# Two LayerNorms of a decoder layer: added products while the statistics run, the order of the first feature pairs, and the last norm as a rounded five-row product

## Chip, cores, metric

One NeuronCore of a Trainium2 chip runs the whole layer in one launch. The metric is the device time of one execution in microseconds (us), as the median of several runs. The engines are TensorE (PE; its weight loads are listed as PEld), VectorE (DVE), ScalarE (ACT), GpSimd (POOL) and SyncE (SP, here a DMA queue only).

## What is computed

A decoder layer on 256 tokens of width 2048 in float32: a token mixer with two branches, then a SwiGLU. Each half ends in a LayerNorm over the 2048 features of a token, and the input of the second half is scaled and shifted feature by feature:

```python
def layer_norm(x, gain, bias):
    mu = xf.mean(-1, keepdims=True)
    var = jnp.square(xf - mu).mean(-1, keepdims=True)
    return ((xf - mu) * lax.rsqrt(var + LN_EPS) * gain + bias).astype(x.dtype)
...
        x = layer_norm(DEEPNORM_ALPHA * x + g1 * y, ln1_g[l], ln1_b[l])
        h = x * (1.0 + sc2) + sh2
        y = swiglu(h, w_ffn_in[l], w_ffn_out[l])
        x = layer_norm(DEEPNORM_ALPHA * x + g2 * y, ln2_g[l], ln2_b[l])
```

## The kernel before

Every float32 product is made of three rounded ones. A weight tile of 128x1024 numbers comes by DMA (`load_w`, line 201), ACT rounds it to `hi` (line 211) and DVE makes `lo = raw - hi` (line 212). PE multiplies hi by the high and the low part of the other operand and lo by its high part (`ws_mm`, lines 289 to 291, weight stationary, 24 products a tile; `xs_unit`, lines 337 to 339, activations stationary). Raw tiles, hi and lo have four buffers each: the conversion of a fifth tile waits until PE is done with the first.

The work is a list of steps. `step` adds one with a weight tile, `do` one without, and `run(3)` goes through the list and issues load and conversion of up to three further tiles ahead of the step that uses them. Behind it a scheduler sets the order of each engine's instructions; `tc.high_priority` lets a piece go ahead of others, and `tc.keep_in_program_order` pins an instruction. At run time every engine takes its own instructions strictly in the order that this gives.

The change touches two places.

The first norm lies between the output projection (`out_unit`, last product of the token mixer) and the first stage of the SwiGLU. `resid` (line 1007) takes a finished block of columns out of PSUM for both halves of the tokens: times the gate (1011), plus alpha times the residual (1012), block statistics (1013). `stats` (1015) joins the blocks' statistics (1020) and takes a reciprocal root with one Newton step (`rsqrt`, lines 347 to 353, of which 348 on ACT). `norm2(g)` (1079) normalizes four features of 128 columns, in pairs: subtract and scale (1084, DVE), four transposes on PE (1090) into one PSUM tile for the pair, then for each feature the scaled and shifted high part (1093, ACT) and the same unrounded (1095, DVE), and one subtraction that gives the low part of the pair (1097). The following stage goes through 4 groups of four features and, in each, through four weight tiles (gate and up, two column blocks each); `norm2(g + 1)` is issued with the first tile of group g.

The end: the last matrix stage ends with `resid` on five blocks of columns (three of 512, two of 256) of the second half's output. After it come `stats` and, for four blocks of 512 columns and both halves of the tokens, a scaling and shift on ACT (1205), times gain (1207) and plus bias (1208) on DVE, of which the last one of each on POOL, and one DMA for each block (1209). Gain and bias of this norm are loaded by SP spread over all 128 partitions, 1 MB each, when the last stage begins (`fo_begin`, lines 1183 and 1184). There also the gate is spread: a transpose (990), a copy (992), and two DMAs on POOL's queue, the write of `rd` (994) and its spread read (995).

Of the kernel before, what the change touches and what calls it, by code (L numbers as in the profile page):

```python
# [10 lines left out]
F32 = mybir.dt.float32  # L11
# [81 lines left out]
def layer(ctx, tc, a, out):  # L93
# [113 lines left out]
    def split_w(raw, kn, cn):  # L207
# [4 lines left out]
        v_.tensor_tensor(lo, raw, hi.bitcast(F32), op=OP.subtract)  # L212
# [50 lines left out]
    def step(w, k0, kn, c0, cn, post):  # L263
        prog.append((lambda: split_w(load_w(w, k0, kn, c0, cn), kn, cn), post))

    def do(fn):
        prog.append((None, fn))

    def run(ahead):
        n = out = 0  # L270
        ready = {}
        for i, (pre, post) in enumerate(prog):
# [734 lines left out]
    def resid(ps, c0, cn, gb, base, dst, st, n):  # L1007
        cc = slice(c0, c0 + cn)
        for h in range(2):
            t = wp.tile([P, 512], F32, tag="acc", name="rt", bufs=2)[:, :cn]  # L1010
            v_.tensor_tensor(t, ps[h], gb[:, cc], op=OP.mult)
            v_.scalar_tensor_tensor(dst[:, h, cc], base[:, h, :], ALPHA, t, op0=OP.mult, op1=OP.add)
            v_.bn_stats(st[:, h, n, :], dst[:, h, cc])

    def stats(st):
        mv = perm.tile([P, 2, 2], F32, tag="mv", name="mv", bufs=2)
        rs = perm.tile([P, 2, 1], F32, tag="lrs", name="lrs", bufs=2)
        with tc.high_priority(offset=400):
            for h in range(2):
                v_.bn_aggr(mv[:, h, :], st[:, h])  # L1020
            rsqrt(rs, *[perm.tile([P, 2, 1], F32, tag="l" + n, name="l" + n) for n in "er"], mv[:, :, 1:2], epsc[:, 1:2])
# [20 lines left out]
    def out_unit(n, c0, cn):  # L1042
# [6 lines left out]
        xs_unit(m_ops, w_o, c0, KT, lambda ps: resid(ps, c0, cn, cur["g1b"], cur["xs"], cur["r"], cur["st"], n), cn)  # L1049
# [10 lines left out]
    def ffn_begin():  # L1060
        halves = [perm.tile([P, 8, 2, S], F32R, tag=tag, name="h2") for tag in ("s0", "s1")]
        cur["h2"] = halves
        for k in range(KT):
            h2.append(halves[k // 8][:, k % 8])
            for x in range(2):
                h2_ops[x].append(h2[k][:, x, :])
        p1.close()
# [7 lines left out]
        cur["mv"], cur["rs"] = stats(cur["st"])  # L1075
# [3 lines left out]
    def norm2(g):  # L1079
        r, mv, rs = cur["r"], cur["mv"], cur["rs"]  # L1080
        for f in range(4 * g, 4 * g + 4, 2):
# [4 lines left out]
            tp = pt.tile([P, 2, S], F32, tag="tp", name="tp")  # L1086
# [4 lines left out]
            t = cur["h2"][f // 8][:, f % 8:f % 8 + 2]  # L1091
# [152 lines left out]
```

## Time and profile before

| | us |
|---|---|
| three runs | 1791.91, 1789.39, 1779.66 |
| their median | 1789.39 |
| the profiled execution | 1785.36 |
| its span, first to last instruction | 1783.6 |
| mean granted clock of TensorE in it | 0.983 of full speed |

The profile is of one execution; its rows give the start from the span's start and the duration in us. Outside the span lie 1.8 us of the profiled execution. A product's duration holds the time in which the next one already runs, so the distance of two starts is what one costs.

### The profile page before, as it was taken

The numbers are of one execution on the slowest core, as the hardware profiler recorded it, in microseconds if no ns is written. First come the engines' busy times: TensorE is split into PE (matmuls) and PEld (weight loads), VectorE is DVE, ScalarE is ACT, GpSimd is POOL, SyncE is SP. The second block draws the span as 40 slices with busy tenths as digits, with TensorE's granted clock in tenths as the row PEclk, the third lists the DMA queues.
The fourth block names the chain that finished last, engine by engine and source line by source line (L and its number), as shares of the span: only waits on it lengthen the run. The fifth ranks groups of instructions, "written<-read, shape, count | busy, mean of one in ns | idle before, by whom it ended". The sixth has DMA issues, their size and how long they took to land.

```text
span 1783.6 us, 28261 instructions
## 1 busy us (share of the span) xinstructions
PE 1686.6 (95%) x11149; PEld 1537.1 (86%) x11149; DVE 1249.9 (70%) x1786; ACT 815.2 (46%) x1118; POOL 49.9 (3%) x68
## 2 busy tenths in 40 slices
PE   3899999999989999899999899999999999999995
PEld 3899999979989788889998899888888888888895
DVE  6899988888856787657875677676666655455454
ACT  3544445667433445336344344544444444433342
POOL 0000000110100001000000000000000000000001
PEclk9999999999999999999999999999999999999998
DMA  9999887666677577876876647777777755765652
GB/s 356 331 339 353 345 310 227 199 196 189 205 238 238 186 237 247 271 239 206 296 265 222 191 129 245 251 252 239 238 246 232 242 193 192 258 197 188 197 185 82
DMA packets 115158, 421.56 MB, mean 236 GB/s; under 512 B 13456, under 2 KB 14384, under 8 KB 109392
## 3 DMA queue, kind: packets, MB, share of 16 engines
q1 hardware_dynamic: 110016, 402.21, 66.7%
q0 software_dynamic: 5008, 17.53, 3.7%
q8 instruction: 88, 1.44, 0.3%
q14 instruction: 46, 0.38, 0.1%
HBM read 412.27 MB, written 7.42 MB: 235 GB/s over the span
## 4 chain that ended last, share of the span: by engine, by line
PE 41%; issue 15%; DMA 8%; DVE 5%; ACT 1%; POOL 0%; POOLq 0%; DVEq 0%; ACTq 0%
PE mm L296 16%; PE mm L300 8%; DMA raw_a<-in_w_ada 4%; DVE lo L212 3%; PE mm L290 3%; PE mm L291 3%; PE mm L289 3%; PE mm L339 2%; PE mm L338 2%; PE mm L337 2%; DMA raw<-in_w_proj_gdn 2%; DMA raw<-in_w_in 1%; ACT hi L211 1%; PE ps L691 1%; DMA rb<-rnd 1%
## 5 line engine op out<-in xcount | busy, mean ns | idle before, releaser
L211 ACT CAST hi<-raw 128x1024 fp32r<-128x1024 f32 (+2 forms) x572 | 582.0, 1020 | 768.7 <-PE mm L339 210.7
L212 DVE TENSOR_TENSOR lo<-raw,hi 128x1024 fp32r<-128x1024 f32 (+2 forms) x572 | 672.8, 1183 | 286.1 <-ACT hi L211 282.1
L289 PE MATMUL mm<-s,hi 128*128 128x256 f32 x1184 | 338.9, 286 | 4.9 <-ACT hi L211 4.7
L291 PE MATMUL mm<-s,lo 128*128 128x256 f32 x1184 | 333.3, 283 | 6.3 <-DVE lo L212 6.2
L290 PE MATMUL mm<-s,hi 128*128 128x256 f32 x1184 | 332.5, 281 | 0.0
L296 PE MATMUL mm<-h,hi 128*128 128x512 f32 x1280 | 319.0, 391 | 0.0
L296 PEld LDWEIGHTS mm<-h,hi 128*128 128x128 f32 x1280 | 228.8, 188 | 39.5
L289 PEld LDWEIGHTS mm<-s,hi 128*128 128x128 f32 x1184 | 225.0, 190 | 10.8 <-ACT hi L211 7.5
L291 PEld LDWEIGHTS mm<-s,lo 128*128 128x128 f32 x1184 | 224.2, 190 | 9.4 <-DVE lo L212 8.5
L290 PEld LDWEIGHTS mm<-s,hi 128*128 128x128 f32 x1184 | 224.8, 190 | 0.4
L300 PEld LDWEIGHTS mm<-h,lo 128*128 128x128 f32 x1280 | 171.1, 188 | 13.2
L300 PE MATMUL mm<-h,lo 128*128 128x256 f32 x1280 | 174.1, 278 | 0.0
L337 PE MATMUL mm<-hi,ach 128*128 128x512 f32 (+1 forms) x440 | 152.6, 347 | 0.0
L338 PE MATMUL mm<-lo,ach 128*128 128x512 f32 (+1 forms) x440 | 152.5, 347 | 0.0
L339 PE MATMUL mm<-hi,acl 128*128 128x512 f32 (+1 forms) x440 | 152.5, 347 | 0.0
L229 DVE CUSTOM_DVE_ANT_0 raw_a<-raw_a,cb,cols 128x1024 f32<-128x1024 f32 x56 | 71.8, 1283 | 77.9 <-DMA raw_a<-in_w_ada 77.9
L229 DVE CUSTOM_DVE_ANT_0 raw_a<-raw_a,cb,ada_half 128x1024 f32<-128x1024 f32 x56 | 71.8, 1283 | 64.8 <-DMA raw_a<-in_w_ada 64.8
L229 DVE CUSTOM_DVE_ANT_0 r<-r,cb,cols 128x2048 f32<-128x2048 f32 x40 | 93.7, 2347 | 14.1 <-DMA r<-in_w_ada 14.1
L337 PEld LDWEIGHTS mm<-hi,ach 128*128 128x128 f32 x440 | 83.3, 189 | 10.4
L339 PEld LDWEIGHTS mm<-hi,acl 128*128 128x128 f32 x440 | 83.3, 189 | 10.4
L338 PEld LDWEIGHTS mm<-lo,ach 128*128 128x128 f32 x440 | 83.3, 189 | 10.1
L338 PE MATMUL mm<-lo,s 128*128 128x512 f32 x192 | 77.0, 401 | 2.2 <-DVE lo L212 2.2
(288 smaller groups left out, 2383.2 us busy)
## 6 DMA issues: line engine op xcount, KB each, us to landing
raw<-in_w_ffn_in SPq DMA_DIRECT2D x176, 512.0 KB, 4.3
raw<-in_w_in SPq DMA_DIRECT2D x168, 512.0 KB, 4.4
raw_a<-in_w_ada SPq DMA_DIRECT2D x112, 512.0 KB, 4.5
raw<-in_w_ffn_out SPq DMA_DIRECT2D x88, 512.0 KB, 4.3
r<-in_w_ada SPq DMA_DIRECT2D x40, 1024.0 KB, 7.6
raw<-in_w_proj_gdn SPq DMA_DIRECT2D x32, 512.0 KB, 4.5
raw<-in_w_out SPq DMA_DIRECT2D x32, 512.0 KB, 4.2
raw<-in_w_in SPq DMA_DIRECT2D x40, 384.0 KB, 5.8
```

Source lines behind the costliest of these rows:

```text
L211: s_.copy(hi, raw)
L212: v_.tensor_tensor(lo, raw, hi.bitcast(F32), op=OP.subtract)
L229: v_.tensor_tensor_reduce(out=raw, in0=raw, in1=cb[:, n * part:n * part + n], scale=1.0, scalar=cols[:, col:col + 1] if first else h, op0= ...
L289: t_.matmul(o, hi[:, i, c], ah, start=(first and i == 0 and t == 0), stop=False)
L290: t_.matmul(o, hi[:, i, c], al, start=False, stop=False)
L291: t_.matmul(o, lo[:, i, c], ah, start=False, stop=(last and i == kn - 1 and t == 1))
L296: t_.matmul(box[t].rearrange("p (u i) -> p u i", u=2), hi[:, i, t * P:(t + 1) * P], both[k0 + i], start=(first and i == 0), stop=False)
L300: t_.matmul(box[t][:, :S], lo[:, i, t * P:(t + 1) * P], both[k0 + i][:, 0, :], start=False, stop=(last and i == kn - 1))
L337: t_.matmul(box[h], xh, hi[:, i, :], start=start, stop=False)
L338: t_.matmul(box[h], xh, lo[:, i, :], start=False, stop=False)
L339: t_.matmul(box[h], xl, hi[:, i, :], start=False, stop=stop)
L691: t_.matmul(ps[:lt.shape[1], n, :], lt, rt, start=True, stop=True)
```

## The change

At the first norm: the last block's `resid` and the statistics behind it are issued as one piece with high priority (`then`). Sixteen products of a finished tile with itself, 512 columns wide, whose result nobody reads, stand on PE behind the last product of the output projection. The two features of a pair get a PSUM tile each, and DVE takes the second feature first. The first two weight tiles are multiplied with the first two features for both tiles (`ws_some`: first everything that needs only high parts, then the rest) before the other two features come in, and `norm2(1)` is issued with the second tile. The fourth tile is loaded and converted no earlier than the first step of the stage (`begun`), with its `lo` pinned (`pin`).

At the second norm: the bias no longer comes spread over the partitions. Gain and bias come once more as rows of 16 x 128, are split into a high and a low part (ACT and DVE), written to DRAM and read back as a tile of five rows: gain high, gain low, bias high, bias low, gain high. Each finished block of columns is multiplied by the gain, once its statistics are taken. At the end the mean times the reciprocal root, negated and split, and ones make a five-row operand for each half of the tokens (two transposes, one copy). One rounded product per half block gives -mean * rs * gain + bias in PSUM, and one DVE step adds r * rs. The last block goes out in two DMAs.

```diff
-    def split_w(raw, kn, cn):
+    def split_w(raw, kn, cn, pin=False):
...
-        v_.tensor_tensor(lo, raw, hi.bitcast(F32), op=OP.subtract)
+        low = v_.tensor_tensor(lo, raw, hi.bitcast(F32), op=OP.subtract)
+        if pin:
+            tc.keep_in_program_order(low)
...
-            while n < len(prog) and (n <= i or out <= ahead):
+            while n < len(prog) and (n <= i or (out <= ahead and prog[n][2] <= i)):
...
-    def resid(ps, c0, cn, gb, base, dst, st, n):
+    def resid(ps, c0, cn, gb, base, dst, st, n, then):
         cc = slice(c0, c0 + cn)
...
+        last = c0 + cn == D
+        with tc.high_priority(offset=400 if last else 0):
+            for h in range(2):
...
+            if last:
+                then(*stats(st))
...
+        keep = pg.tile([P, 512], F32, tag="gd", name="keep")
+        for _ in range(16):
+            t_.matmul(keep, cur["mh"][0][:, 0, :P], cur["mh"][0][:, 0:2, :], start=True, stop=True)
         p1.close()
...
+            t = cur["h2"][f // 8][:, f % 8:f % 8 + 2]
+            tps = []
             for i in range(2):
+                tps.append(pt.tile([P, S], F32, tag="tp", name="tpn"))
                 for h in range(2):
-                    t_.transpose(tp[:, i, h * P:(h + 1) * P], r[:, h, (f + i) * P:(f + i + 1) * P], ident)
+                    t_.transpose(tps[i][:, h * P:(h + 1) * P], r[:, h, (f + i) * P:(f + i + 1) * P], ident)
...
+                j = 1 - i
+                v_.tensor_scalar(hf[:, j, :], tps[j], sa[:, 0, f + j:f + j + 1], sa[:, 1, f + j:f + j + 1],
                                  op0=OP.mult, op1=OP.add)
...
+    def ws_some(ps, hi, lo, some, first, last):
+        for i in some:
+            for t in range(2):
+                o, c = ps[:, t * S:(t + 1) * S], slice(t * P, (t + 1) * P)
+                t_.matmul(o, hi[:, i, c], h2_ops[0][i], start=(first and i == some[0] and t == 0), stop=False)
+                t_.matmul(o, lo[:, i, c], h2_ops[0][i], start=False, stop=False)
+        for i in some:
+            for t in range(2):
+                t_.matmul(ps[:, t * S:(t + 1) * S], hi[:, i, t * P:(t + 1) * P], h2_ops[1][i], start=False, stop=False)
...
-                if n == 0 and g < 3:
-                    norm2(g + 1)
-                ws_mm(pss[n], h2_ops, hi, lo, 4 * g, 4, g == 0, g == 3)
...
+                held.append((hi, lo))
+                ws_some(pss[n], hi, lo, (0, 1), True, False)
+                if n:
+                    norm2(1)
+                    for m in range(2):
+                        ws_some(pss[m], *held[m], (2, 3), False, False)
...
-        dma.dma_start(b1[:, 1, :], a["ln2_b"][0].partition_broadcast(P))
...
+        row = wp.tile([KT, 2, P], F32, tag="acc", name="row", bufs=2)
+        for i, v in enumerate(("ln2_g", "ln2_b")):
+            sdma.dma_start(row[:, i, :], a[v].rearrange("o (k p) -> (o k) p", p=P))
+        hl = wp.tile([KT, 2, 2, P], F32R, tag="acc", name="hl", bufs=2)
+        split(hl[:, 0], hl[:, 1], row)
+        hld = dr.tile([4, D], F32R, name="hld")
+        sdma.dma_start(hld.rearrange("x (k p) -> k x p", p=P), hl.rearrange("k x v p -> k (x v) p"))
+        rows = cur["rows"] = k3.tile([5, D], F32R, name="rows")
+        sdma.dma_start(rows[0:4], hld)
+        sdma.dma_start(rows[4:5], hld[0:1])
...
+            resid(ps, c0, cn, cur["g2b"], r[:, :, cc], r, cur["st"], n, finish)
+            for h in range(2):
+                v_.tensor_tensor(r[:, h, cc], r[:, h, cc], cur["g"][:, cc], op=OP.mult)
...
+    def finish(mv, rs):
...
+        v_.scalar_tensor_tensor(nm, mv[:, :, 0:1], -1.0, rs, op0=OP.mult, op1=OP.mult)
+        v_.tensor_copy(z[:, :, 0:3:2], nm.to_broadcast([P, 2, 2]))
+        v_.tensor_tensor(z[:, :, 4:5], nm, z[:, :, 0:1].bitcast(F32), op=OP.subtract)
+        tp = pt.tile([P, 512], F32, tag="tp", name="tpm")
+        for h in range(2):
+            t_.transpose(tp[0:5, h * P:(h + 1) * P], z[:, h, :].bitcast(F32), ident)
...
+        s_.copy(zt, tp[0:5, :S].rearrange("p (h i) -> p h i", h=2))
...
-            s_.activation(r[:, h, cc], r[:, h, cc], AF.Identity, bias=nm[:, h], scale=rs[:, h])
-            e = g_ if (n == 3 and h == 1) else v_
-            e.tensor_tensor(r[:, h, cc], r[:, h, cc], b1[:, 0, cc], op=OP.mult)
-            e.tensor_tensor(r[:, h, cc], r[:, h, cc], b1[:, 1, cc], op=OP.add)
...
+            t_.matmul(ps, cur["zt"][:, h], cur["rows"][:, cc], start=True, stop=True)
+            v_.scalar_tensor_tensor(r[:, h, cc], r[:, h, cc], rs[:, h], ps, op0=OP.mult, op1=OP.add)
```

Three places show what the scheduler makes of it. In the names, `lo<-raw,hi` is the low part of a weight tile, `rt`, `r`, `st`, `mv` and `lrs` are the steps of a block and of its statistics, and `tp` or `tpn` is a transposed pair or feature. A line number that begins a row is that of its own kernel, those of after being later by what was added above.

DVE at the first norm, before, from the second half of the last block to the third pair:

```order
L1012 SCALAR_TENSOR_TENSOR r<-xs,rt 128x256
L1020 BN_AGGR mv<-st_9708 128x2
L212 TENSOR_TENSOR lo<-raw,hi 128x1024
L1013 BN_STATS st_9708<-r 128x6
L1020 BN_AGGR mv<-st_9708 128x2
...
L1097 TENSOR_TENSOR h_10446<-hf_10474,h_10446 128x2x256
L1084 TENSOR_SCALAR r<-r,mv,lrs 128x256 x2
L1095 TENSOR_SCALAR hf_10487<-tp,sa 128x256 x2
L1097 TENSOR_TENSOR h_10446<-hf_10487,h_10446 128x2x256
L1084 TENSOR_SCALAR r<-r,mv,lrs 128x256 x2
```

And DVE at the same place after:

```order
L1016 SCALAR_TENSOR_TENSOR r<-xs,rt 128x256
L1025 BN_AGGR mv<-st_9708 128x2
L1017 BN_STATS st_9708<-r 128x6
L1025 BN_AGGR mv<-st_9708 128x2
...
L1107 TENSOR_TENSOR h_10453<-hf_10484,h_10453 128x2x256
L1092 TENSOR_SCALAR r<-r,mv,lrs 128x256 x2
L1105 TENSOR_SCALAR hf_10498<-tpn,sa 128x256 x2
L1107 TENSOR_TENSOR h_10453<-hf_10498,h_10453 128x2x256
L212 TENSOR_TENSOR lo<-raw,hi 128x1024 x2
L1092 TENSOR_SCALAR r<-r,mv,lrs 128x256 x2
```

The low part of the fourth tile has moved from within the statistics to behind the second pair, where another one follows it, ahead of the third pair's normalization.

ACT where the last matrix stage begins, before (`ach` is the high part of the last SwiGLU activations):

```order
L1114 COPY up<-mm 128x256 x2
L211 CAST hi<-raw 128x1024
L217 CAST ach<-up 128x512
L211 CAST hi<-raw 128x1024 x65
```

And ACT there after:

```order
L1124 COPY up<-mm 128x256 x2
L211 CAST hi<-raw 128x1024
L219 CAST ach<-up 128x512
L219 CAST hl<-row 16x256
L211 CAST hi<-raw 128x1024 x65
```

The split of the two rows stands ahead of all conversions of the stage but the first of these.

DVE at the last block of the last norm, before:

```order
L1011 TENSOR_TENSOR rt<-mm,b_15073 128x256
L1012 SCALAR_TENSOR_TENSOR r<-r,rt 128x256
L1013 BN_STATS st_15084<-r 128x6
L1020 BN_AGGR mv<-st_15084 128x2
L347 TENSOR_SCALAR le<-mv,epsc 128x2
```

And DVE there after (`b_15099` is the gain):

```order
L1015 TENSOR_TENSOR rt<-mm,b_15098 128x256
L1238 TENSOR_TENSOR r<-r,b_15099 128x256
L1016 SCALAR_TENSOR_TENSOR r<-r,rt 128x256
L1017 BN_STATS st_15121<-r 128x6
L1025 BN_AGGR mv<-st_15121 128x2
L1238 TENSOR_TENSOR r<-r,b_15099 128x256
L349 TENSOR_SCALAR le<-mv,epsc 128x2
```

Both multiplications by the gain of the last block stand within the chain that ends in the reciprocal root.

## Rows read from the trace of the kernel before

**Rows 1.** The page: the span, and from its first section TensorE's busy time in us (share of the span) and number of instructions.

```profile
span 1783.6 us, 28261 instructions
...
PE 1686.6 (95%) x11149; PEld 1537.1 (86%) x11149; DVE 1249.9 (70%) x1786; ACT 815.2 (46%) x1118; POOL 49.9 (3%) x68
```

**Rows 2.** Busy time by window (us from the span's start): length, then PE, PEld, DVE, ACT and POOL busy us (instructions), PE's granted clock, the DMA engines' busy share and GB/s. The first norm in three stretches, the last matrix stage, the end.

```profile
1018.95:1024.30 5.35, 0.17 (x3) 0.01 (x1) 4.84 (x16) 1.25 (x2) 0.00 (x0) 0.81 0.59 194
1024.30:1032.50 8.20, 6.29 (x26) 5.45 (x27) 3.23 (x7) 2.03 (x4) 0.00 (x0) 0.50 0.00 2
1032.50:1079.90 47.40, 46.97 (x393) 46.04 (x392) 35.61 (x54) 24.61 (x32) 0.00 (x0) 1.00 0.53 167
1531.00:1764.00 233.00, 233.00 (x1278) 203.78 (x1276) 113.49 (x109) 86.80 (x83) 0.51 (x1) 1.00 0.57 185
1764.00:1783.60 19.60, 0.18 (x2) 0.00 (x0) 11.65 (x27) 5.96 (x9) 6.03 (x2) 0.56 0.28 107
```

**Rows 3.** PE's timeline around the first norm: start, duration, line, operation, out<-in, shape, count, and in brackets the engine's idle time ahead of it with what ended it. The last row is the first product of the stage that follows.

```profile
1018.83 0.28 PE L339 MATMUL mm<-hi,ml 128*128 128x256 f32 x1
1024.30 1.23 PE L1090 MATMUL tp<-cst,r 128*128 128x128 f32 x4 [5.18 <-DVE r L1084]
1026.17 1.23 PE L289 MATMUL mm<-h,hi 128*128 128x256 f32 x4 [0.66 <-ACT h L1093]
1028.66 0.58 PE L290 MATMUL mm<-h,hi 128*128 128x256 f32 x1 [1.26 <-DVE h L1097]
...
1031.17 0.41 PE L291 MATMUL mm<-h,lo 128*128 128x256 f32 x1
1031.38 0.41 PE L289 MATMUL mm<-h,hi 128*128 128x256 f32 x1
...
1033.09 0.28 PE L290 MATMUL mm<-h,hi 128*128 128x256 f32 x1
1033.21 0.28 PE L291 MATMUL mm<-h,lo 128*128 128x256 f32 x1
...
1079.90 1.32 PE L296 MATMUL mm<-h,hi 128*128 128x512 f32 x5
```

**Rows 4.** DVE's timeline at the same place.

```profile
1020.48 1.16 DVE L212 TENSOR_TENSOR lo<-raw,hi 128x1024 fp32r<-128x1024 f32 x1
1021.56 0.42 DVE L1013 BATCH_NORM_STATS2 st<-r 128x6 f32<-128x256 f32 x1
...
1023.83 0.73 DVE L1084 TENSOR_SCALAR r<-r,mv,lrs 128x256 f32<-128x256 f32 x2
1026.16 0.54 DVE L1095 TENSOR_SCALAR hf<-tp,sa 128x256 f32<-128x256 f32 x1 [1.59 <-ACT h L1093]
1027.33 0.55 DVE L1095 TENSOR_SCALAR hf<-tp,sa 128x256 f32<-128x256 f32 x1 [0.63 <-ACT h L1093]
1027.91 0.69 DVE L1097 TENSOR_TENSOR h<-hf,h 128x512 fp32r<-128x512 f32 x1
```

**Rows 5.** ACT's timeline at the same place.

```profile
1025.56 0.56 ACT L1093 ACTIVATE h<-tp,sa 128x256 fp32r<-128x256 f32 x1 [2.76 <-PE tp L1090]
1026.73 0.56 ACT L1093 ACTIVATE h<-tp,sa 128x256 fp32r<-128x256 f32 x1 [0.61 <-DVE hf L1095]
...
1036.61 1.05 ACT L211 CAST hi<-raw 128x1024 fp32r<-128x1024 f32 x1 [0.19 <-PE mm L290]
```

**Rows 6.** PE's timeline at an earlier gap in dense work, and the window around it with the columns of rows 2.

```profile
134.57 0.39 PE L291 MATMUL mm<-s,lo 128*128 128x256 f32 x1 [1.57 <-DVE lo L212]
...
130.00:137.00 7.00, 5.43 (x46) 5.23 (x45) 6.31 (x8) 2.17 (x3) 0.00 (x0) 1.00 0.86 297
```

**Rows 7.** Where the last matrix stage begins: POOL's timeline (DMA issues), ACT's, PE's (the first product of the stage), and the time from issue to landing of line 994's two DMAs.

```profile
1523.78 0.51 POOL L994 DMA_DIRECT2D rd<-rw  x1 [587.09 <-DVE rw L992]
1530.96 0.55 POOL L995 DMA_DIRECT2D b<-rd  x1 [6.67 <-ACT hi L211]
...
1526.83 1.05 ACT L211 CAST hi<-raw 128x1024 fp32r<-128x1024 f32 x1 [1.19 <-issue]
...
1521.05 0.48 PE L337 MATMUL mm<-hi,ach 128*128 128x512 f32 x1
...
DMA to landing us min/median/max: 3.9/5.3/6.6
```

**Rows 8.** The end: DVE's and POOL's timelines, the four DMAs of the output (line 1209; durations of the issue in ns, first and last start, time from issue to landing), and a window with the columns of rows 2.

```profile
1766.01 0.23 DVE L347 TENSOR_SCALAR le<-mv,epsc 128x2 f32<-128x2 f32 x1
...
1767.50 0.16 DVE L1201 SCALAR_TENSOR_TENSOR nm<-mv,lrs 128x2 f32<-128x2 f32 x1
...
1769.88 1.28 DVE L1207 TENSOR_TENSOR r<-r,b 128x512 f32<-128x512 f32 x2
...
1773.54 4.77 POOL L1207 TENSOR_TENSOR r<-r,b 128x512 f32<-128x512 f32 x1 [242.03 <-ACT r L1205]
1778.38 1.26 POOL L1208 TENSOR_TENSOR r<-r,b 128x512 f32<-128x512 f32 x1
...
L1209 SPq DMA_DIRECT2D out<-r x4: 372/384/398, 1771.8 to 1779.7; - x4
...
DMA to landing us min/median/max: 2.7/2.8/2.8
...
1773.00:1774.00 1.00, 0.00 (x0) 0.00 (x0) 1.00 (x2) 0.45 (x1) 0.46 (x1) 0.50 1.02 387
```

More of the change, by code (lines that the diff above doesn't have):

```diff
@@ L261, in layer, with step @@
     prog = []
-    def step(w, k0, kn, c0, cn, post):
-        prog.append((lambda: split_w(load_w(w, k0, kn, c0, cn), kn, cn), post))
+    def step(w, k0, kn, c0, cn, post, begun=0, pin=False):
+        prog.append((lambda: split_w(load_w(w, k0, kn, c0, cn), kn, cn, pin), post, begun))
     def do(fn):
-        prog.append((None, fn))
+        prog.append((None, fn, 0))
     def run(ahead):
@@ L271, in run @@
         ready = {}
-        for i, (pre, post) in enumerate(prog):
-            while n < len(prog) and (n <= i or out <= ahead):
+        for i, (pre, post, _) in enumerate(prog):
+            while n < len(prog) and (n <= i or (out <= ahead and prog[n][2] <= i)):
                 if prog[n][0]:
@@ L1005, in layer @@
     do(out_begin)
-    def resid(ps, c0, cn, gb, base, dst, st, n):
+    def resid(ps, c0, cn, gb, base, dst, st, n, then):
         cc = slice(c0, c0 + cn)
[L1009 to L1013, printed above, removed]
+        last = c0 + cn == D
+        with tc.high_priority(offset=400 if last else 0):
+            for h in range(2):
+                t = wp.tile([P, 512], F32, tag="acc", name="rt", bufs=2)[:, :cn]
+                v_.tensor_tensor(t, ps[h], gb[:, cc], op=OP.mult)
+                v_.scalar_tensor_tensor(dst[:, h, cc], base[:, h, :], ALPHA, t, op0=OP.mult, op1=OP.add)
+                v_.bn_stats(st[:, h, n, :], dst[:, h, cc])
+            if last:
+                then(*stats(st))
     def stats(st):
@@ L1017, in stats @@
         rs = perm.tile([P, 2, 1], F32, tag="lrs", name="lrs", bufs=2)
[L1018 to L1021, printed above, removed]
+        for h in range(2):
+            v_.bn_aggr(mv[:, h, :], st[:, h])
+        rsqrt(rs, *[perm.tile([P, 2, 1], F32, tag="l" + n, name="l" + n) for n in "er"], mv[:, :, 1:2], epsc[:, 1:2])
         return mv, rs
@@ L1129, in wide_unit @@
             step(w_fi, k, 4, c0, 256, post)
+    def ws_some(ps, hi, lo, some, first, last):
[7 more added lines that the diff above has]
+                t_.matmul(ps[:, t * S:(t + 1) * S], hi[:, i, t * P:(t + 1) * P], h2_ops[1][i], start=False, stop=False)
+    begun, held = len(prog), []
     for g in range(4):
@@ L1133, in post @@
             def post(hi, lo, g=g, n=n):
-                if n == 0 and g < 3:
-                    norm2(g + 1)
-                ws_mm(pss[n], h2_ops, hi, lo, 4 * g, 4, g == 0, g == 3)
-            step(w_fi, 4 * g, 4, o, 256, post)
+                if g or n > 1:
+                    if n == 0 and g < 3:
+                        norm2(g + 1)
+                    ws_mm(pss[n], h2_ops, hi, lo, 4 * g, 4, g == 0, g == 3)
+                    return
+                held.append((hi, lo))
[4 more added lines that the diff above has]
+                        ws_some(pss[m], *held[m], (2, 3), False, False)
+            step(w_fi, 4 * g, 4, o, 256, post, begun if (g, n) >= (0, 3) else 0, (g, n) == (0, 3))
     def ln1_affine():
@@ L1180, in fo_begin @@
         b0 = perm.tile([P, 2, D], F32, tag="s0", name="b0")
[L1181 removed]
+        b1 = perm.tile([P, 1, D], F32, tag="s1", name="b1")
         bcast_row(5, b0[:, 0, :])
         dma.dma_start(b1[:, 0, :], a["ln2_g"][0].partition_broadcast(P))
[L1184 to L1185 removed]
+        cur["g2b"], cur["g"] = b0[:, 0, :], b1[:, 0, :]
+        k3 = cur["k3"]
+        row = wp.tile([KT, 2, P], F32, tag="acc", name="row", bufs=2)
[8 more added lines that the diff above has]
+        sdma.dma_start(rows[4:5], hld[0:1])
+        z = cur["z"] = k3.tile([P, 2, 5], F32R, name="z")
+        v_.memset(z.bitcast(F32), 1.0)
         cur["st"] = perm.tile([P, 2, 5, 6], F32, tag="stt", name="st2", bufs=2)
```

34 lines of the change are left out of this document (18 added, 16 removed).

## The prediction

> **What bounds the kernel now.** I read the page's busy times first, then windows, then the engines' timelines around both norms. TensorE (PE) is busy 1686.6 of 1783.6 us [rows 1], and in the last matrix stage it never stops (233.00 of 233.00 us) while VectorE (DVE) is busy 113.49 [rows 2]: what does not hold PE up there costs nothing. So only the two places where PE does stop can pay.
>
> At the first norm the last product of the output projection starts at 1018.83 and PE sits idle 5.18 us until the row statistics and the first normalization are done [rows 3]. Its granted clock falls in that gap (mean 0.81), is 0.50 from 1024.3 to 1032.5, so the lower level of 1.2 GHz, and 1.00 (2.4 GHz) after [rows 2]. Products start every 0.21 us at the lower clock (1031.17 to 1031.38) and every 0.12 at the higher (1033.09 to 1033.21) [rows 3]. In the slow stretch PE waits twice more: 0.66 us for ScalarE (ACT) and 1.26 us for DVE [rows 3].
>
> At the end PE is out of work at 1764.0 and the span ends at 1783.6: 19.6 us of DVE, ACT, POOL and one transfer [rows 2, 8].
>
> **The first norm, step by step.** From 1032.5 to 1079.9 PE is held up hardly at all: 47.40 us with 393 instructions [rows 2], 0.1206 us each, transposes included. The whole stage has 16 weight tiles x 24 products + 32 transposes = 416 instructions, so 50.2 us at that pace. It takes 1079.90 - 1018.95 = 60.95 [rows 2, 3]. The most that can be won here is 10.8 us.
>
> Statistics: before, the low part of a weight tile (1020.48, 1.16 us) stands between two steps of the chain [rows 4]; the change moves it behind the second pair of features. The chain ends 1.08 us earlier (next statistic at 1020.48 and not 1021.56): the first L1084, at 1023.83 before [rows 4], starts at 1022.75. Its two halves end at 1023.15 and 1023.48.
>
> The 16 repeated products are 512 columns wide, about 0.23 us each by twice the step of a 256-wide one [rows 3], so 3.7 us: from 1018.95 to 1022.65, before the first transpose can start (1023.2). They cost nothing and leave PE idle 0.55 us in place of 5.18.
>
> First pair: transposes end at 1023.82 and 1023.93. Before, ACT and DVE read one bank in turn: 1025.56, 1026.16, 1026.73, 1027.33, then the low part at 1027.91 [rows 4, 5], four reads in 2.35 us. With a bank each they read side by side, two turns of 0.57: 1023.87 to 1025.05, low part until 1025.8. PE's first product can start at 1024.5 (before 1026.17), and what waited for the low part (1028.66 before) at 1025.8 [rows 3]. From 1024.5 there are 16 products that need only the high parts of two features (1.9 us at full clock), so the wait for the low part is covered, and 8 more that reach until 1027.4. The second pair (normalized at 1025.7 to 1026.45, transposed by 1027.0, high part of its first feature at 1027.6, low parts at 1028.9) arrives 0.1 to 0.2 us late.
>
> At full clock the rest is 412 x 0.1206 = 49.7 us from 1024.5: 1074.2 without further waits. There are some: two tiles are now finished side by side, so the first tile's buffers come free at about 1029.5 and the next conversion waits for them, as at 1036.61 before [rows 5]; on DVE two conversions (1.2 us each [rows 4]) now stand ahead of the third pair's normalization. Stepping through the pairs with these durations, the third waits about 0.3, its low part 0.4, and each of the last four 0.3 to 0.5: 1.6 with the second pair's. Ends: 0, if all stays covered, and 4 (six pairs behind half a conversion each). I take 1.6: the stage ends at 1075.8, **4.1 us earlier** (bounds 1.7 and 5.7 with the clock kept up).
>
> Does the clock stay up? With the added products the gaps are 0.55 us before the transposes and 0.6 after them. A gap of 1.57 us at 134.57 in dense work left the granted clock at 1.00 [rows 6]. The Trainium skill (TensorE: Matmul & The Clock Gate, Part 4: PE-mode transpose) says that transposes do not count as work for the clock gate. By that rule the gap would be one of 1.85 us (1022.65 to 1024.5). No row here separates transposes from products; before, four transposes at 1024.30 and a few products left the clock at 0.50 until 1032.5 [rows 2, 3], which fits the rule and also fits plain thinness of work. I keep this as a rival.
>
> **The start of the last matrix stage.** New small loads of the gain and the bias (rows of 16 x 128) go over POOL's queue, and ACT and DVE split them. ACT is in order: the split stands ahead of the conversion that ran at 1526.83 before [rows 7]. Behind it all later conversions queue, and for these waits PE. The second row's load is issued behind the write of rd, at 1524.3; that write, of 8 KB like each of these rows, took 6.6 us to land [rows 7], so ACT could go on at about 1531.3, 4.5 us late. PE takes up that tile, the sixth (the first started at 1521.05), five tiles of 12 products x 0.23 us later, at 1534.8; 1.05 and 1.2 us of conversion must fit ahead of it, so the copy may end at 1532.4 at the latest. Cover of 1.1 us: I count 0. The Trainium skill (DMA: Bandwidth & Descriptors, Anatomy of one DMA, SWDGE path) gives about 2.0 us plus bytes over bandwidth for such a transfer. By that figure the row would land at about 1526.3 and ACT would not wait; the 6.6 us here is over three times that, and the row decides. The ten multiplications by the gain (DVE, two per block) lie in a stage where DVE has 119 us to spare [rows 2]: 0, but for the last two.
>
> **The end.** Added to the chain: the last block's two multiplications, one between the halves (+0.27) and one ahead of the epsilon step at 1766.01 (+0.22; of 0.42 each, part lies in the gaps between dependent steps) [rows 8]. nm starts at 1768.0 (before 1767.50). Then two small DVE steps (+0.2 each, end 1768.55), two transposes at the low clock (0.3 apart, 0.4 long: 1769.3), ACT's copy of 5x256 out of PSUM (at most the 0.56 of a 128x256 read [rows 5]; bounds 0.2 and 0.56, I take 0.45): 1769.8, one five-row product of 512 columns at the low clock (0.43 + 0.2 to drain): 1770.45. Then eight DVE steps of 128x512, 0.60 apart as L1207's [rows 8]: the last ends at 1775.35. Before, it was POOL's 1779.64 [rows 8], because a 4.77 us and a 1.26 us step on POOL ended last.
>
> The transfers are late next. Before, the four of 512 KB were issued 2.6 us apart on average (1771.8 to 1779.7) and landed 2.8 after their issue [rows 8]: 1.35 us of data at 387 GB/s (1773 to 1774 [rows 8]) and 1.45 around them. Now 2.1 MB are issued from 1771.75 (end of the second of the eight steps) to 1775.4, closer together than they can be moved: 5.4 us of data and 1.45 around them, so they land at 1778.6. From the last landing to the span's end there were 1.1 us (1779.7 + 2.8 against 1783.6): 1779.7. For joints between five transfers I take 1779.9, **3.7 us earlier**. Bounds: 5.0, if the last 256 KB finds no queue (1775.4 + 2.1 + 1.1), and 1.9, if each of the four joints costs 0.45 more.
>
> **Sum** against the profiled execution: 1785.4 - 4.1 - 3.7 = 1777.6 us. That execution lies 4.0 below the median of the three runs (1789.39; 1779.66 to 1791.91); the four known times average 1786.6, so 1778.8. I forecast 1779.
>
> **Rivals.**
> (a) The clock falls all the same, because the added products end before the statistics do. For: two pauses close to each other from 1022.65 to 1024.5. Against: 16 dense products right ahead and the kept clock at 134.57 [rows 6]. Price: 8.2 us at half clock, as in the slow stretch before [rows 2], but with PE busy: 4.1 us lost. 1785.4 - 3.7 = 1781.7.
> (b) The new order starves PE later in the stage: 4 us of waits in place of 1.6, ACT and DVE being strictly in order. For: conversions ahead of normalizations. Against: DVE is busy 35.61 of 47.40 us there [rows 2]. 1780.
> (c) All goes through: no late waits, transfers overlap: 5.7 + 5.0, 1774.7.
> (d) Slower: the row of the bias lands late. Place: ACT's split at the start of the last stage. Price: each us beyond 1532.4 holds PE up one us, and beyond some 5 us the clock falls as at 1018.83 and takes another 4. Landing after 13.3 us, twice that of rd: 5.6 + 4.1 = 9.7 lost, 1.9 more than is won: 1787.3. It decides from about 11.5 us on. Against: one broadcast of 1 MB less is in flight, and rd's 6.6 us is the nearest row.
>
> **Chances.** Forecast 0.52, (a) 0.16, (b) 0.14, (c) 0.14, (d) 0.04. A measurement of this kernel tells about 1% (17.9 us) from no change; all cases lie within it, and only (c) met by a low run, or (d) far beyond its point, gets out: faster 0.08, same 0.89, slower 0.03. The range goes from (c) less the 5.7 us by which the fastest run lay under the profiled one, 1769, to (a) or (d) plus the 4 us of the median: 1788.
>
> **What would show it.** Right: idle time ahead of the first transpose under 1 us; granted clock 1.00 from 1018 to the end of the stage; ACT's and DVE's reads of one pair starting together; first 512-wide product of the next stage some 55 to 58 us after the last one of the output projection (before 61.1); PE without a gap near the sixth tile of the last stage; last DVE step 11.2 to 11.7 us after the last product (before POOL, 15.7); landing about 3.1 us behind it. Wrong: a slow stretch after the added products, an ACT wait for the row's load that PE feels, or transfers that leave gaps at the end.

## The result: 0.5% less time, 5.0 us of it at the first norm and 3.6 at the end

The changed kernel takes 1777.01 us (median of 13 runs, 1773.09 to 1783.01), the kernel before 1786.41 on the same chip (13 runs, 1779.66 to 1791.91): ratio 0.9950, 95% interval 0.9938 to 0.9963. The profiled execution took 1777.62 us with a span of 1775.85; before 1785.36 and 1783.59. The forecast for the median was 1779.

The two spans differ by 7.74 us, made up so. The last product of the output projection starts 0.87 later, by small differences in the stages ahead, whose code is the same. From its last product to the first product of the wide stage it takes 1075.77 - 1019.70 = 56.06 us in place of 61.06. The stages from there to the last product take 0.04 less. From the last product to the end of the span it takes 1775.85 - 1759.72 = 16.13 in place of 19.70. So +0.87 - 5.00 - 0.04 - 3.57 = -7.74. The medians differ by 9.4, and the interval runs from 6.6 to 11.1.

The page, against [rows 1]: TensorE is busy 10.5 us more and is still the engine that bounds.

```profile
PE 1697.1 (96%) x11175; PEld 1544.0 (87%) x11175; DVE 1253.0 (71%) x1794; ACT 811.1 (46%) x1112; POOL 46.2 (3%) x71
```

Windows, against [rows 2] and with its columns: the gap behind the output projection, the first pair, the rest of that stage, the last matrix stage, the end.

```profile
1019.70:1024.05 4.35, 3.94 (x20) 2.95 (x18) 3.80 (x16) 1.26 (x2) 0.00 (x0) 1.00 0.41 121
1024.05:1025.36 1.31, 0.76 (x5) 0.40 (x5) 0.79 (x4) 0.56 (x1) 0.00 (x0) 1.00 0.00 0
1025.36:1075.77 50.41, 49.84 (x413) 48.69 (x413) 41.00 (x64) 26.49 (x34) 0.00 (x0) 1.00 0.55 177
1531.00:1755.00 224.00, 224.00 (x1219) 195.52 (x1218) 114.42 (x112) 85.54 (x82) 1.01 (x2) 1.00 0.58 184
1759.72:1775.85 16.13, 5.26 (x13) 2.44 (x11) 9.26 (x25) 0.56 (x2) 0.00 (x0) 0.58 0.35 131
```

The granted clock is 1.00 in all three windows of the norm, where before it was 0.50 for 10.24 us, 8.2 of them from 1024.3 on. In the first one PE is now busy 3.94 of 4.35 us, and the last matrix stage still has no pause.

PE's timeline at the norm, against [rows 3].

```profile
1019.70 0.28 PE L341 MATMUL mm<-hi,ml 128*128 128x256 f32 x1
1019.82 3.82 PE L1075 MATMUL keep<-mh 128*128 128x512 f32 x16
1024.05 0.77 PE L1100 MATMUL tpn<-cst,r 128*128 128x128 f32 x4 [0.41 <-DVE r L1092]
1025.36 0.38 PE L1145 MATMUL mm<-h,hi 128*128 128x256 f32 x1 [0.55 <-ACT h L1102]
...
1075.77 0.40 PE L298 MATMUL mm<-h,hi 128*128 128x512 f32 x1
```

The 5.18 us of idle time are down to 0.41, and the first product starts 5.65 us behind the last one of the output projection (before 7.34). The 1.26 us wait for the low part is gone.

VectorE's timeline and then ScalarE's, against [rows 4] and [rows 5].

```profile
1023.58 0.74 DVE L1092 TENSOR_SCALAR r<-r,mv,lrs 128x256 f32<-128x256 f32 x2
...
1024.85 1.03 DVE L1105 TENSOR_SCALAR hf<-tpn,sa 128x256 f32<-128x256 f32 x2 [0.52 <-PE tpn L1100]
1026.03 0.69 DVE L1107 TENSOR_TENSOR h<-hf,h 128x512 fp32r<-128x512 f32 x1
...
1029.78 1.22 DVE L212 TENSOR_TENSOR lo<-raw,hi 128x1024 fp32r<-128x1024 f32 x1
1031.82 1.23 DVE L212 TENSOR_TENSOR lo<-raw,hi 128x1024 fp32r<-128x1024 f32 x1 [0.82 <-ACT hi L211]
```

```profile
1024.74 1.25 ACT L1102 ACTIVATE h<-tpn,sa 128x256 fp32r<-128x256 f32 x2 [2.19 <-PE tpn L1100]
...
1030.74 1.05 ACT L211 CAST hi<-raw 128x1024 fp32r<-128x1024 f32 x1 [1.60 <-PE mm L1149]
```

ScalarE reads the pair from 1024.74 and VectorE from 1024.85, side by side; before, their four reads took turns. The first L1092 starts 3.88 behind the last product, L1084 did at 5.00. Further on, ScalarE's conversion at 1030.74 waits for PE (1.60 us ahead of that row), and two low parts of weight tiles on VectorE (1029.78, 1031.82) stand ahead of the third pair.

The start of the last matrix stage, against [rows 7]: POOL's issues, ScalarE's timeline, PE's first product of the stage.

```profile
1519.63 0.49 POOL L996 DMA_DIRECT2D rd<-rw  x1 [428.16 <-DVE rw L994]
1520.11 0.49 POOL L1217 DMA_DIRECT2D row<-in_ln_b  x1
...
1525.42 0.41 ACT L219 CAST hl<-row 16x256 fp32r<-16x256 f32 x1 [3.96 <-DMA row<-in_ln_b]
1525.73 2.00 ACT L211 CAST hi<-raw 128x1024 fp32r<-128x1024 f32 x2
...
1516.87 0.48 PE L339 MATMUL mm<-hi,ach 128*128 128x512 f32 x1
```

The row of the bias lands 5.2 us after its issue. ScalarE stands still for it (3.96 us), and both conversions behind it run at once after 1525.73. PE waits for nothing from 1500 to 1757.

The end, against [rows 8]: VectorE; then PE, ScalarE and the last two output transfers (line 1265, time from issue to landing).

```profile
1760.47 0.41 DVE L1238 TENSOR_TENSOR r<-r,b 128x256 f32<-128x256 f32 x1
...
1761.92 0.36 DVE L1238 TENSOR_TENSOR r<-r,b 128x256 f32<-128x256 f32 x1
...
1763.67 0.16 DVE L1245 SCALAR_TENSOR_TENSOR nm<-mv,lrs 128x2 f32<-128x2 f32 x1
...
1766.16 5.35 DVE L1263 SCALAR_TENSOR_TENSOR r<-r,lrs,mm 128x512 f32<-128x512 f32 x8 [1.92 <-PE mm L1262]
```

```profile
1764.29 0.59 PE L1250 MATMUL tpm<-cst,z 128*5 128x128 f32 x2 [4.29 <-DVE z L1247]
1765.33 4.40 PE L1262 MATMUL mm<-rows,zt 5*128 5x512 f32 x8 [0.45 <-ACT zt L1252]
...
1764.92 0.36 ACT L1252 CAST zt<-tpm 5x256 fp32r<-5x256 f32 x1 [2.27 <-PE tpm L1250]
...
L1265 SPq DMA_DIRECT2D out<-r x2: 345/454/564, 1770.9 to 1771.5; - x2
...
DMA to landing us min/median/max: 3.1/3.1/3.1
```

nm starts 3.95 us behind the last product (before 3.60), the first of the eight steps 6.44 behind it. The eighth ends at 1771.51, +11.79, where POOL's last step ended at +15.74. The last transfer lands 3.1 later, and 1.2 after that the span ends.

### The profile page after: what moved, and what is told of

The parts are those of the page before. It is cut to its first block, busy times and chain, and to the rows that moved or that the text cites. A ratio compares the mean times of both kernels' runs of the same rounds, so it can differ in the third digit from the quotient of the medians.

```text
span 1775.9 us, 28332 instructions
## 1 busy us (share of the span) xinstructions
PE 1697.1 (96%) x11175; PEld 1544.0 (87%) x11175; DVE 1253.0 (71%) x1794; ACT 811.1 (46%) x1112; POOL 46.2 (3%) x71
## 4 chain that ended last, share of the span: by engine, by line
PE 74%; DMA 11%; DVE 8%; issue 4%; ACT 2%; POOL 0%; DVEq 0%; ACTq 0%; SPq 0%; POOLq 0%
PE mm L298 16%; PE mm L302 8%; PE mm L339 8%; PE mm L341 8%; PE mm L340 8%; PE mm L293 6%; PE mm L291 6%; PE mm L292 6%; DMA raw_a<-in_w_ada 4%; DVE lo L212 4%; DMA raw<-in_w_in 3%; DMA raw<-in_w_proj_gdn 2%; ACT hi L211 1%; PE ps L693 1%; DMA r<-in_w_ada 1%
```

## Experiments

Two lengths are read from every profile: the *norm stage* (last product of the output projection to first product of the wide stage) and the *end* (last product to the span's end). The ratio is to the kernel before on the same chip. Its intervals are 2 to 4 us wide to either side, so costs of 1 to 3 us are read from the stages and not from the medians.

| kernel | norm stage | granted clock at 0.50: from (behind the last product), for | end | ratio (95%) |
|---|---|---|---|---|
| before | 61.06 | +3.48, 10.24 | 19.70 | 1 |
| changed | 56.06 | none | 16.13 | 0.9950 (0.9938-0.9963) |
| no_keep | 57.20 | +5.10, 3.41 | 16.12 | 0.9962 (0.9941-0.9983) |
| old_stats | 57.18 | none | 16.13 | 0.9967 (0.9954-0.9981) |
| one_bank | 60.76 | +22.97, 3.41 | 15.92 | 0.9987 (0.9972-1.0003) |
| old_order | 57.12 | none | 15.95 | 0.9978 (0.9961-0.9995) |
| no_keep_old_order | 59.95 | +3.21, 10.24 | 16.13 | 0.9964 (0.9950-0.9977) |
| before_keep | 61.07 | +8.47, 6.83 | 19.69 | 0.9992 (0.9975-1.0009) |
| before_banks | 60.68 | +3.50, 10.24 | 19.69 | 1.0005 (0.9986-1.0023) |
| before_dve_end | 60.36 | +3.01, 10.24 | 18.56 | 0.9987 (0.9970-1.0004) |
| keep_transp | 56.06 | none | 15.88 | one run |
| keep4 | 58.14 | +4.05, 6.83 | 16.14 | one run |
| pin_end | 56.06 | none | 15.79 | 0.9935 (0.9917-0.9954) |
| pin_no_keep | 57.31 | +5.33, 3.41 | 15.59 | 0.9959 (0.9944-0.9974) |

The norm of before_dve_end is the one of the kernel before: 60.36 and 61.06 show how far two profiles of the same code lie apart there (0.7). The changed norm repeats better: 56.06 in the changed kernel and in pin_end, 57.20 and 57.31 in no_keep and pin_no_keep, which have the same code there. The end of the changed kernel stands unchanged in eight of the profiles and takes 15.88 to 16.14: nm starts at +3.95 in each, but the first of the eight steps at +6.18 to +6.45. It is the earlier (+6.18 to +6.26) in the three in which the clock falls at +4.79 to +5.49, and the later where it falls at +2.42 to +4.61.

**The repeated products taken out (no_keep).**

```diff
-        for _ in range(16):
-            t_.matmul(keep, ...)
```

> The changed kernel without its 16 repeated products (L1075); nothing else is taken out. Measured is the stage from the last product of the output projection to the first product of the wide stage: 61.06 us before, 56.06 after. Theory (the repeated products hold the clock, the order does the rest): the first product still starts at +5.65, since VectorE's chain sets it; TensorE has no work for some 4.4 us, and the granted clock falls near +3.5 for some 10 us, as in the kernel before. Some 7 to 8 us of that lie behind the start of the products, which then run at half speed beside waits that take part of it: the stage becomes 58.5 to 60 us, the span 2.5 to 4 longer. Rival (order and banks did it, the repeated products only fill idle time): 56.1 within 0.5, whatever the clock's record shows.

57.20: between the two. Windows with the columns of [rows 2]: the slow stretch and the rest of the stage.

```profile
1026.36:1029.78 3.42, 2.98 (x14) 2.88 (x14) 2.33 (x5) 1.05 (x2) 0.00 (x0) 0.50 0.00 0
1029.78:1078.47 48.69, 48.01 (x402) 46.93 (x401) 40.00 (x59) 25.91 (x33) 0.00 (x0) 1.00 0.59 188
```

The first product starts at +5.64, as with them. The clock falls, but while it is low PE is busy 2.98 of 3.42 us, and it is back after that. The repeated products are worth 1.14 here, and 1.25 in pin_no_keep against pin_end (57.31, 56.06), not the 2.5 to 4 that I expected.

**The old place of the statistics (old_stats).**

```diff
-        with tc.high_priority(offset=400 if last else 0):
+        with tc.high_priority(offset=400 if last and then is finish else 0):
...
+        cur["mv"], cur["rs"] = stats(cur["st"])
         norm2(0)
...
-            step(w_fi, ..., begun if (g, n) >= (0, 3) else 0, (g, n) == (0, 3))
+            step(w_fi, ..., 0, False)
```

> The changed kernel with the statistics of the first norm where the kernel before had them (no raised priority for the last residual block, low halves of the weights not held back). Theory: the first scaling step of VectorE moves from +3.88 back towards +5.0, the products start 1.1 later, and the gap behind the repeated products grows from 0.41 to about 1.5; the clock holds; the stage is 57.2 us. Rival (the clock falls in the longer gap, which makes the earlier statistics a condition of the repeated products' effect): the granted clock falls near +7.5 and the stage is 59 to 61 us. Second rival: products start 1.1 later but the waits behind them shrink by as much, and the stage stays 56.1 within 0.4.

57.18, first product at +6.77: the theory. The pause behind the repeated products grows to 1.52 and the clock stays at 1.00, so the earlier statistics are worth their own 1.12 and are no condition for the rest.

**One bank for a pair (one_bank).**

```diff
+            tp = pt.tile([P, 2, S], F32, tag="tp", name="tpn")
+            tps = [tp[:, 0], tp[:, 1]]
...
-                tps.append(pt.tile([P, S], F32, tag="tp", name="tpn"))
```

> The changed kernel with one PSUM tile for the two features of a pair, as before, instead of one each. Theory (a bank per feature lets ScalarE and VectorE read side by side): ScalarE's and VectorE's first readings follow one another again, the low part of the first pair is ready 0.8 to 1.2 later, and the tiles come free later for the next transposes: the first product starts 0 to 0.6 later and the stage is 57 to 58 us. Rival (only the earlier products matter): the readings change place but PE has products to do meanwhile, and the stage stays 56.1 within 0.4.

60.76: the direction of the theory, but a cost of 4.70 where it gave 0.9 to 1.9. The first product is only 0.22 later (+5.87). The loss comes at the third pair: ScalarE's timeline, then VectorE's with PE's wait.

```profile
1040.02 0.57 ACT L1102 ACTIVATE h<-tpn,sa 128x256 fp32r<-128x256 f32 x1 [0.51 <-PE tpn L1100]
1041.95 1.04 ACT L211 CAST hi<-raw 128x1024 fp32r<-128x1024 f32 x1 [1.36 <-PE mm L292]
1042.90 0.56 ACT L1102 ACTIVATE h<-tpn,sa 128x256 fp32r<-128x256 f32 x1
```

```profile
1039.21 2.36 DVE L212 TENSOR_TENSOR lo<-raw,hi 128x1024 fp32r<-128x1024 f32 x2
1041.48 0.54 DVE L1105 TENSOR_SCALAR hf<-tpn,sa 128x256 f32<-128x256 f32 x1
1043.03 1.23 DVE L212 TENSOR_TENSOR lo<-raw,hi 128x1024 fp32r<-128x1024 f32 x1 [1.01 <-ACT hi L211]
1044.17 0.54 DVE L1105 TENSOR_SCALAR hf<-tpn,sa 128x256 f32<-128x256 f32 x1
...
1044.95 0.69 DVE L1107 TENSOR_TENSOR h<-hf,h 128x512 fp32r<-128x512 f32 x1
...
1045.69 0.58 PE L292 MATMUL mm<-h,hi 128*128 128x256 f32 x1 [2.25 <-DVE h L1107]
```

The four reads of one tile take turns: ScalarE at 1040.02, VectorE at 1041.48, ScalarE at 1042.90, VectorE at 1044.17. Ahead of each turn a weight conversion of 1.04 to 1.23 us stands in that engine's queue, so a pair takes 4.7 us from the first read to the end of the last; PE waits 2.25 for its low part, and there the clock falls too. All of PE's pauses in the stage sum to 4.66 us (changed kernel 1.52); the other 1.6 of the 4.7 are products at half clock. In the trace the second reader waits until the first is done (in [rows 4], too, VectorE's 1.59 us are ended by ScalarE's step), though neither writes what the other reads. What two readers at once would do to each other in one bank is not measured here; the cost is that of the turns.

**The old order of the first products (old_order), and both undone (no_keep_old_order).**

```diff
-                if g or n > 1:
+                if True:
```

> The changed kernel with the products of the first two weight tiles in the old order (all four features of a tile, then the next tile) and the second group's norm where it stood. Theory: the products of features 2 and 3 stand in TensorE's queue ahead of work that is ready, so TensorE waits 1 to 2 us more for their transposes and scalings; the stage is 57 to 58.5 us. Rival (the repeated products alone, by the clock): the stage stays 56.1 within 0.5.

57.12: the theory. PE waits 0.69 at +7.07 for the first low part, and the clock stays up.

> The changed kernel without the repeated products and with the old order of the first products; earlier statistics and a bank per feature stay. Alone, the two edits gave 57.20 and 57.12. Theory (what TensorE does while the clock is low decides how long it stays low: without a pause 3.41 us, with the old waits 10.24 as before): the stretch at 0.50 is 6.8 us or longer and the stage 59 to 60.5 us. Rival (both add up, the length of the slow stretch is that of the run without repeated products): a stretch of 3.41 us and a stage of 58.3 within 0.4.

59.95, with the clock low for 10.24 us: the theory. The slow stretch as a window:

```profile
1023.67:1033.91 10.24, 8.38 (x35) 7.54 (x36) 7.06 (x17) 2.26 (x4) 0.00 (x0) 0.50 0.00 0
```

Now PE is busy only 8.38 of the 10.24 us. So the repeated products are worth 2.83 with the old order (59.95 - 57.12) and 1.14 with the new one (57.20 - 56.06); the order is worth 2.75 without them and 1.06 with them. What makes the slow stretch short is not fully separated: in the two profiles with the new order it also began later (+5.1 and +5.3, in place of +3.0 to +3.5).

**Single parts added to the kernel before (before_keep, before_banks).**

```diff
+        keep = pg.tile([P, 512], F32, tag="gd", name="keep")
+        for _ in range(16):
+            t_.matmul(keep, cur["mh"][0][:, 0, :P], cur["mh"][0][:, 0:2, :], start=True, stop=True)
         p1.close()
```

> The kernel before with nothing but the 16 repeated products added ahead of its first norm. Measured again is the stage from the last product of the output projection to the first product of the wide stage (61.06 before, 56.06 after). Theory (the repeated products hold the clock whatever the order): the first product still starts at +7.3; the 6.35 us of work that ran at the lower clock take 3.2 less, of which up to 1 goes into longer waits: the stage is 58 to 59 us. Rival (the waits of the old order, 1.5 behind the repeated products, 0.65 and 1.26 soon after, drop the clock all the same): a stretch at 0.50 appears and the stage is 60.5 to 61.5 us.

61.07, nothing won: my theory fell. PE's timeline, and the slow stretch as a window.

```profile
1027.61 0.87 PE L1093 MATMUL tp<-cst,r 128*128 128x128 f32 x4 [1.52 <-DVE r L1087]
1029.13 0.72 PE L289 MATMUL mm<-h,hi 128*128 128x256 f32 x4 [0.66 <-ACT h L1096]
...
1031.62 0.58 PE L290 MATMUL mm<-h,hi 128*128 128x256 f32 x1 [1.76 <-DVE h L1100]
...
1030.61:1037.44 6.83, 5.82 (x27) 5.82 (x28) 3.80 (x9) 1.13 (x2) 0.00 (x0) 0.50 0.00 0
```

The repeated products carry the clock over the first gap, but longer pauses follow (1.52, 0.66, 1.76), and the clock falls at +8.47. The old order of the products alone does not do that: in old_order, which has it, the pauses are 0.40, 0.55 and 0.69 and the clock stays up. What before_keep lacks besides is the earlier statistics and the bank per feature. With the old statistics alone (old_stats: 1.52, then 0.55) the clock stays up as well, so no single one of the three is shown to be the condition. The 1.76 is 0.5 longer than the same wait before, which fits products that reach it sooner at full clock.

before_banks takes `norm2` of the changed kernel (the `tps` lines) into the kernel before, and nothing else.

> The kernel before with a bank per feature in the first norm, read side by side, and nothing else. Theory (the alternating reads of one bank made the low parts late): the first product starts at +6.8 instead of +7.34, the wait of 1.26 for the low part shrinks below 0.6; the clock falls as before, and the stage is 59 to 60.3 us (61.06 and, in a second profile of the same code there, 60.36). Rival (the banks help only with the new order): 60.4 to 61.1.

60.68. The first product is earlier (+6.92) and the wait for the low part shrinks from 1.26 to 0.51, as the theory has it; but the clock falls as before, and the stage lies in the rival's range, between two profiles of the old code. So neither part brings anything measurable alone.

**What the added work must be (keep_transp, keep4).** Twenty-eight transposes in place of the sixteen products; and four products in place of sixteen (`range(4)`).

```diff
-        for _ in range(16):
-            t_.matmul(keep, ...)
+        for _ in range(28):
+            t_.transpose(keep[:, :P], cur["mh"][0][:, 0, :P].bitcast(F32), ident)
```

> The changed kernel with 28 transposes of 128x128 in place of the 16 repeated products, so TensorE is as long at work ahead of the statistics' end but with transposes alone. Theory (work of either kind holds the clock): no stretch at 0.50 within 20 us, stage 56.1 within 0.4. Rival (transposes do not hold it, so the gap is as long as without them, 5.6 us): a stretch at 0.50 begins between +3 and +6.5 behind the last product of the output projection, and the stage is 57 to 59 us, as without the repeated products (57.20). The Trainium skill (TensorE: Matmul & The Clock Gate, Part 4: PE-mode transpose) says the latter.

56.06, the clock never below 1.00: PE's timeline and windows.

```profile
1015.75 3.22 PE L1075 MATMUL keep<-cst,mh 128*128 128x128 f32 x28
1019.97 0.76 PE L1100 MATMUL tpn<-cst,r 128*128 128x128 f32 x4 [1.00 <-DVE r L1092]
1021.28 0.38 PE L1145 MATMUL mm<-h,hi 128*128 128x256 f32 x1 [0.55 <-ACT h L1102]
...
1015.70:1019.30 3.60, 3.27 (x30) 3.03 (x29) 3.09 (x13) 1.25 (x2) 0.00 (x0) 1.00 0.45 146
1021.30:1071.70 50.40, 49.83 (x413) 48.64 (x414) 41.62 (x64) 26.59 (x34) 0.00 (x0) 1.00 0.57 182
```

Transposes alone held it in this profile, over 3.2 us of them and a pause of 1.00. The Trainium skill's sentence that transposes do not count as PE-busy in the same way (TensorE: Matmul & The Clock Gate, Part 4: PE-mode transpose) would have had it fall as in no_keep; here the measurement decides.

> The changed kernel with 4 repeated products instead of 16: they end near +1.1, and TensorE is idle some 3.2 us before the first transpose. Theory (the length of the pause decides): a stretch at 0.50 begins between +3 and +6.5, stage 57 to 58.5 us. Rival (any work in the gap will do): the clock stays 1.00 and the stage is 56.1 within 0.4.

58.14, as in the theory: with a pause of 3.12 us the clock falls at +4.05 and stays low for 6.83.

Each of the two is a single profile, and a single profile of the clock can mislead. Near 788 us, in code that all these kernels share, TensorE pauses once ahead of eight small products. PE's row and the window, in keep_transp and then in old_order:

```profile
785.06 2.08 PE L693 MATMUL ps<-z,UU 128*128 128x128 f32 x8 [2.15 <-DVE z L702]
...
784.90:788.30 3.40, 3.24 (x15) 3.24 (x16) 2.52 (x4) 1.58 (x3) 0.00 (x0) 0.50 0.88 308
```

```profile
789.53 1.16 PE L693 MATMUL ps<-z,UU 128*128 128x128 f32 x8 [3.35 <-DVE z L702]
...
780.00:800.00 20.00, 16.25 (x139) 15.85 (x138) 12.88 (x17) 6.93 (x13) 0.00 (x0) 1.00 0.79 264
```

The clock fell in a pause of 2.15 us and stayed up through one of 3.35. So the length of one pause did not decide there, and keep4 alone does not show that it does at the norm. That work in the gap counts rests on more profiles: the clock held across it in all six of the changed kernel's versions with sixteen products or 28 transposes, and in all six profiles without added work it fell within 5.4 us of the last product.

**The end (before_dve_end, pin_end, pin_no_keep).**

```diff
-            e = g_ if (n == 3 and h == 1) else v_
+            e = v_
```

> The kernel before with the last two steps of its last norm on VectorE instead of POOL. From the last product to the span's end: 19.70 us before, 16.13 after. Theory (POOL's two steps end 1.26 behind what two more steps of VectorE, 0.60 apart, would): 18.4 us; the other 2.3 us of the changed kernel's end come from eight steps in place of sixteen. Rival (POOL's step was the whole delay, the transfers do the rest): 16.0 to 17.0 us. Second rival (the transfers set the end): 19.4 to 19.8.

18.56: the theory. POOL's two steps cost the kernel before 1.14. The other 2.43 of the 3.57 are left for the new form by subtraction; no run has the new form alone.

```diff
-                v_.tensor_tensor(r[:, h, cc], r[:, h, cc], cur["g"][:, cc], op=OP.mult)
+                late = v_.tensor_tensor(r[:, h, cc], r[:, h, cc], cur["g"][:, cc], op=OP.mult)
+                if n == 4:
+                    tc.keep_in_program_order(late)
```

> The changed kernel with the last block's two multiplications by the gain put behind the statistics (into the 1.9 us in which VectorE waits for the five-row product) instead of between their steps. Theory (they stand on the chain that ends last): the row of -mean times scale (nm) starts at +3.60 behind the last product instead of +3.95, everything behind it is 0.35 earlier, and the span ends 15.7 to 15.8 behind the last product (16.13). Rival (the output transfers set the end): nm earlier, the end 16.1 within 0.1.

15.79: the theory. VectorE's timeline (last product at 1758.85):

```profile
1762.46 0.16 DVE L1247 SCALAR_TENSOR_TENSOR nm<-mv,lrs 128x2 f32<-128x2 f32 x1
...
1762.94 0.75 DVE L1238 TENSOR_TENSOR r<-r,b 128x256 f32<-128x256 f32 x2
1764.94 5.36 DVE L1265 SCALAR_TENSOR_TENSOR r<-r,lrs,mm 128x512 f32<-128x512 f32 x8 [1.25 <-PE mm L1264]
```

nm is back at +3.60, and both multiplications (0.75 us) run where VectorE waits for the product anyway. The first of the eight steps starts at +6.09, and at +5.88 in pin_no_keep, whose clock falls later (+4.77, in pin_end +2.80); each is 0.3 to 0.4 ahead of the profiles of the changed end in which the clock falls at a like time. So the 0.34 by which the end is shorter stands, although profiles of one end differ by 0.26. By its median, 1773.78 us of 6 runs, this version is ahead of both kernels; its interval overlaps with that of the changed kernel.

> The version with the late multiplications behind the statistics, without the repeated products. Theory: as between the changed kernel with and without them, the granted clock falls in the gap, for 3.41 us if nothing pauses after the first product, and the stage is 57 to 58.5 us; the median is 1 to 2 us above that of the version with them (1773.78). Rival (the repeated products are worth nothing as a median of runs): within 0.7 of it.

Norm stage 57.31, clock low for 3.41 us: the theory. The medians (1777.10 of 12 runs against 1773.78 of 6 on another chip) differ by 3.3, more than the forecast 1 to 2 and than the 1.25 that the stage shows; the rest is not explained.

## Why the prediction was right, and which terms were not

**Statistics (1.08 earlier), first product at 1024.5, so +5.67, pause of 0.55 ahead of the transposes.** Measured 1.12, +5.65 and 0.41; old_stats shows that the 1.12 arrive whole.

**The clock.** It stayed up, as forecast, over a pause of 0.41 and one of 0.55. Rival (a), the clock falling all the same, had the wrong price: I took 8.2 us at half clock with PE busy, 4.1 lost. Where it did fall with the new order, it cost 1.14 and 1.25, and 2.08 in keep4. And I gave the repeated products alone the credit for the clock; before_keep shows that without the other parts they bring nothing.

**Late waits: the mis-sized term.** From the first product on I took 49.7 us of work and 1.6 of waits; measured 50.41, so 0.7. That is why the norm gave 5.0 and not 4.1. Rival (b), 4 us of waits, is out for this kernel. one_bank shows what such a starved stage looks like: 4.7 us. I had worked out the bank per feature at the first pair alone, where it moves PE by 0.22, and it earns its keep at the third pair, where conversions stand in both queues.

**Start of the last stage.** ScalarE went on at 1525.73, 8.86 behind the stage's first product; forecast 10.3 (1531.3 - 1521.05). The row landed in 5.2 us where I used the 6.6 of rd. The fixed 2.0 us of the Trainium skill (DMA: Bandwidth & Descriptors, Anatomy of one DMA, SWDGE path) was further off. PE did not wait, so the cover that I claimed held, and rival (d) did not happen. Two figures of this part of the prediction do not follow from their own terms: the latest end of the copy is 1534.8 - 1.05 - 1.2 = 1532.6, not 1532.4, and with the clock falling only after 5 us of waits, (d) would decide from a landing of about 12.7 us on, not 11.5.

**The end: -3.57, forecast -3.7.** Three terms missed and partly cancel. The two multiplications on the chain cost 0.35 (forecast 0.49; pin_end confirms 0.35 by taking them off). The eight steps come 0.66 apart (forecast 0.60 from L1207, which has another operation and reads SBUF, where these read PSUM; which of the two makes the difference is not tested), so the last ends at +11.79 in place of +11.45. And from there to the span's end it takes 4.34 in place of 4.55: the landing of 3.1 was as forecast, and the 0.2 that I added for joints between the transfers did not appear. The price of POOL's steps was in the sum only as part of the whole; it is 1.14.

**Sum.** 1777.6 on the profiled execution came out as 1777.62, partly by luck: the norm won 0.9 more, and the stages ahead of it took 0.87 more. For the median, 1779 was forecast and 1777.01 measured, inside the range. Its upper end of 1788 is not what its terms give: (a) plus 4 is 1785.7, (d) plus 4 is 1791.3.

## What to carry over

Work that only keeps the clock up paid here where the pauses behind the gap were short (0.40, 0.55 and 0.69 us in old_order, worth 2.83); where longer ones followed (1.52, 0.66 and 1.76 in before_keep), the clock fell a few us later and nothing was won. So look first at what comes behind the gap. Two engines that read one PSUM tile in turns lose at each turn what stands ahead in their queues: a tile each moved the first product by 0.22 us at the first pair, and at the third, with conversions in both queues, its lack cost PE 3 us of waits. At the end of a kernel, look for steps that stand between links of the last chain but are needed later, and pin them into the chain's next wait.

## What I had not expected

- Undoing parts of the norm one at a time costs 1.14 + 1.12 + 4.70 + 1.06 = 8.0 us, all together 5.0; adding one at a time to the kernel before wins 0 (before_keep) and 0.4 (before_banks), within the 0.7 between two profiles of the same code.
- The low stretch of the clock is not fixed: 3.41, 6.83 or 10.24 us at this norm, and in code that all these kernels share, near 728 us, 3.41 in the profile of before and of the changed kernel and 10.24 in no_keep and pin_end.
- Transposes alone held the granted clock at 1.00 (one profile).
